# Decoder step on one core: the sample's own cached keys and values read through GpSimd's queue

## The chip, the cores and the metric

The kernel runs on one core of a Trainium2 chip. The core has TensorE (PE in the profile: matmuls and transposes), VectorE (DVE), ScalarE (ACT), GpSimd (POOL) and SyncE (SP, which here only issues transfers), and 16 DMA engines that move data between HBM and on-chip memory. The metric is the device time of one execution in microseconds (us); lower is better.

## The reference, cut to what matters

One inference step of one decoder layer for two groups of tokens that share all weights: a prompt of 1024 tokens and a sample group of 8 sequences with 8 new tokens each. The normalised input goes through one projection, which gives a pooling branch, queries, keys, values and two gates. Attention has three head groups of four heads of 64, with (window, dilation) = (128, 1), (512, 4) and (2048, 16). For a sample token it is

```
idx = Lw + arange(T)[:, None] - arange(band + 1)[None, :] * dil
kg, vg = k_full[:, idxc], v_full[:, idxc]
s = einsum('bthd,btjhd->bthj', q, kg) * HEAD_DIM ** -0.5
p, lse = masked_softmax_stats(s, valid)
out = einsum('bthj,btjhd->bthd', p, vg)
```

where `k_full` and `v_full` are the cached rows followed by the new ones. In the third head group (dilation 16) the 8 new tokens of a sequence share no key: each reads its own 128 cached rows, one in 16. The three groups' outputs are combined by their softmax denominators, mixed with the pooling branch through the gates, projected, and followed by a squared-ReLU MLP. The outputs are both groups' tokens and all updated caches.

## The kernel before, in words

Matrices are f32, split into a high and a low part; a product is three matmul passes. The program runs in this order: the pooling projection, attention (head group index g = 2, then 1, then 0), the gates, the output projections, the MLP. Each head group takes the projection in blocks of 128 tokens: blocks 0 to 7 are the prompt, block 8 is the sample group. For blocks 1 to 5, PE computes queries and keys together (`pqk`, 512 columns) and then values (`pv`); for the others each apart (`pq`, `pk`, `pv`). While PE goes on, a block's queries and keys are normalised in a relay: ACT squares them (L643), DVE sums the squares (L644, `ms`), POOL adds epsilon (L650) and takes the power -1/2 (L651, `mr`), ACT scales (L656), and about one block later PE transposes the result (L672, `tqg1b` for g = 1, `tqg0b` for g = 0).

The third head group's sample attention has no shared keys and does not go to PE. It is done tile by tile while head groups 1 and 0 occupy PE: 16 tiles of keys (`pck`), a softmax, 16 tiles of values (`pcv`). A tile is 128 partitions by 4 cached rows by 256 numbers. `piece` reads it in two halves of 64 partitions (L846); POOL multiplies it in four operations (L856) with the queries or the softmax weights; DVE reduces keys (L869) or adds values (L894, L895). Tiles alternate between two buffers, so tile n + 2 can be read only when DVE has finished tile n. `sample_own_keys` asks for the next tile ahead of multiplying the present one; the multiplications also wait for a matmul that has been traced before them and for the last L651. A tile is worked on after the middle and after the end of a block's PE work, two a block.

At the end, the sums are added into `osm` (L899), combined with the other groups' (L763) and given to PE (L1096). Later POOL also issues 96 cache-to-cache copies (L2115), from 454.9 us on.

PE's order is the order of the program. The order on the other engines and queues is chosen by a scheduler when the kernel is built, from its own estimate of all durations; each engine then runs its list strictly in order, so an instruction that waits holds all behind it. Before the change SyncE's queue issues all transfers but L2115, among them the shared heads' cached keys (`kt`, `keys`, L923 and L927) and the weights (`raw`, L123 and L127).

Of the kernel before, what the change touches and what calls it, by code (L numbers as in the profile page):

```python
# [37 lines left out]
def decoder_step(ctx, tc, i, o):  # L38
    nc = tc.nc
    v_, s_, g_, t_ = nc.vector, nc.scalar, nc.gpsimd, nc.tensor  # L40
    dma = nc.sync.dma_start
# [7 lines left out]
    def rr(p, shape, dt, name, tag, bufs):  # L49

        n = turn[p, tag] = turn.get((p, tag), -1) + 1
        return p.tile(shape, dt, name=name, tag=f"{tag}.{n % bufs}", bufs=1)
# [787 lines left out]
    def piece(kv, j, name):  # L840
        t = rr(sp1, [P, KPC, 256], F32, name=f"pc{name}", tag="pc", bufs=2)
        src = i["cache_kv3"]
        for hf in range(2):
            a = bass.AP(tensor=src.tensor, offset=src.offset + (64 * hf + j) * DIL[2] * NB * 512 + kv * 256,
                        ap=[[512, NT * NB], [DIL[2] * NB * 512, KPC], [1, 256]])
            dma(t[64 * hf:64 * hf + 64], a)  # L846
        return t

    def sample_own_keys(qs, wq):
# [5 lines left out]
        def times(out, *others):  # L855
            ins = g_.tensor_tensor(out, *others, op=ALU.mult)  # L856
            behind_pe(ins)
            behind_pe(ins, last_norm[0])

        loaded = [piece(0, 0, "k0")]  # L860
        yield
        behind_pe(v_.scalar_tensor_tensor(qs[:, :256], wq, HD ** -0.5, qs[:, :256], op0=ALU.mult, op1=ALU.mult))
        for j in js:
            t = loaded.pop()
            loaded.append(piece(0, j + KPC, f"k{j + KPC}") if j + KPC < 64 else piece(1, 0, "v0"))
            for n in range(KPC):
                times(t[:, n], t[:, n], qs[:, :256])
            yield
            behind_pe(v_.tensor_reduce(sc[:, j:j + KPC, :].rearrange("p i h -> p (i h)"),  # L869
                                       t.rearrange("p i (h d) -> p (i h) d", h=4), axis=AX.X, op=ALU.add))  # L870
# [14 lines left out]
        for j in js:  # L885
            t = loaded.pop()
            if j + KPC < 64:
                loaded.append(piece(1, j + KPC, f"v{j + KPC}"))
            for n in range(KPC):
                tv = t[:, n].rearrange("p (h d) -> p h d", h=4)  # L890
                times(tv, tv, sc[:, j + n, :].unsqueeze(2).to_broadcast([P, 4, HD]))
            yield
            if j:
                behind_pe(v_.tensor_tensor(t[:, :2], t[:, :2], t[:, 2:], op=ALU.add))  # L894
                v_.tensor_tensor(st2, st2, t[:, :2], op=ALU.add)  # L895
            else:
                behind_pe(v_.tensor_tensor(st2, t[:, :2], t[:, 2:], op=ALU.add))
# [461 lines left out]
    def row_tile(n, name):  # L1359
        return rr(rows_p, [P, H], F32, name=f"g{n}_{name}", tag=f"g{n}", bufs=2)  # L1360
# [149 lines left out]
    for n, (f, a) in enumerate(order):  # L1510
# [5 lines left out]
        t = row_tile(1 + a, f)  # L1516
# [700 lines left out]
```

## Time and profile before

| what | us |
|---|---|
| median of 3 runs | 1408.12 |
| the runs | 1403.95 to 1409.54 |
| the profiled execution | 1403.42 |
| its span, first to last instruction | 1401.6 |
| PE busy | 1392.2 |
| POOL busy | 236.2 |
| L846 issues on SyncE's queue | 64, from 167.0 to 366.0 |

The page counts an engine as busy while an instruction of it runs. A row of the timeline view has the start, the duration, the engine, the line, the operation and the tiles (output <- inputs); "x4" says how many instructions the row merges, and brackets hold the idle time ahead of it and what ended that. SPq is SyncE's queue; its durations are those of issuing, not of moving data. Waits are listed with their total, their number and the longest.

### The profile page before, as it was taken

What the parts mean: (1) busy time and instruction counts of PE and PEld (TensorE: products, weight loads), DVE (VectorE), ACT (ScalarE), POOL (GpSimd) and SP (SyncE); (2) the same over time, 40 slices, a digit from 0 to 9 for tenths busy, and PEclk for the clock granted to TensorE, in tenths of its full rate; (3) what the DMA queues carried; (4) which work ended last, traced back from release to release, by engine and by line L of the source; (5) the groups of instructions that cost most, each with busy time, mean ns of one, the idle gap of its engine ahead of it and who ended that gap; (6) DMA issues with size and microseconds to landing.
All of it is one profiled execution on the core that took longest, in us unless ns stands there. A gap on an engine that the chain in (4) does not pass through costs nothing.

```text
span 1401.6 us, 29306 instructions
## 1 busy us (share of the span) xinstructions
PE 1392.2 (99%) x11101; PEld 1342.7 (96%) x11101; DVE 954.3 (68%) x1714; ACT 754.5 (54%) x1778; POOL 236.2 (17%) x330
## 2 busy tenths in 40 slices
PE   9999999999999999999999999999999999999998
PEld 8988977887999999999999999999999999999998
DVE  7788744776776767875568677665665686664565
ACT  8557766687765323563336455555554544444443
POOL 0722266475500000000010000000000000000100
PEclk9999999999999999999999999999999999999999
DMA  6322788745477767965368668856758987777684
GB/s 215 117 90 102 220 228 215 216 127 144 120 254 232 253 216 250 319 227 179 130 203 285 227 221 269 269 200 210 249 189 287 325 272 261 234 243 231 206 260 168
DMA packets 184540, 303.57 MB, mean 217 GB/s; under 512 B 26567, under 2 KB 90509, under 8 KB 182350
## 3 DMA queue, kind: packets, MB, share of 16 engines
q1 hardware_dynamic: 181326, 258.04, 58.4%
q0 software_dynamic: 3072, 43.65, 9.8%
q8 instruction: 87, 1.43, 0.4%
q14 instruction: 55, 0.45, 0.1%
HBM read 231.55 MB, written 113.73 MB: 246 GB/s over the span
## 4 chain that ended last, share of the span: by engine, by line
PE 93%; DMA 2%; POOL 2%; DVE 1%; ACT 1%; issue 0%; SPq 0%; DVEq 0%; POOLq 0%
PE pz L1297 24%; PE pd L2075 24%; PE pg L1297 12%; PE ph L200 7%; PE pqk L200 5%; PE pab L1297 5%; PE pv L200 4%; PE a L328 3%; PE pq L200 1%; PE pk L200 1%; POOL pcv L856 1%; PE sg0b L689 1%; PE pog0b L722 1%; PE tpg0b L708 1%; POOL mr L651 0%; DMA ts_d<-ts 0%
## 5 line engine op out<-in xcount | busy, mean ns | idle before, releaser
L2075 PE MATMUL pd<-places 128*128 128x272 f32 x2688 | 331.7, 287 | 0.0
L2075 PEld LDWEIGHTS pd<-places 128*128 128x128 f32 x2688 | 331.6, 188 | 0.0
L116 ACT ACTIVATE places<-raw_d 128x544 fp32r<-128x544 f32 (+1 forms) x176 | 110.7, 646 | 162.7 <-DMA raw_d<-z_d 51.4
L117 DVE TENSOR_TENSOR places<-raw_d,places 128x544 fp32r<-128x544 f32 (+1 forms) x176 | 122.6, 712 | 92.4 <-ACT places L116 90.6
L2115 POOL DMA_DIRECT2D out_kv_sample_dram<-in_cache_kv_dram x96 | 47.2, 492 | 790.7 <-ACT places L116 580.9
L1297 PE MATMUL pz<-act,places 128*128 128x280 f32 (+1 forms) x1080 | 139.4, 287 | 0.0
L1297 PEld LDWEIGHTS pz<-act,places 128*128 128x128 f32 x1080 | 135.9, 188 | 0.0
L200 PE MATMUL ph<-act,places 128*128 128x280 f32 (+1 forms) x768 | 96.6, 287 | 0.0
L200 PEld LDWEIGHTS ph<-act,places 128*128 128x128 f32 x768 | 96.0, 188 | 0.1
L1297 PE MATMUL pg<-act,places 128*128 128x264 f32 (+1 forms) x576 | 75.6, 288 | 0.0
L1297 PEld LDWEIGHTS pg<-act,places 128*128 128x128 f32 x576 | 72.6, 188 | 0.6 <-issue 0.3
L1297 PE MATMUL pz<-places,apart 128*128 128x264 f32 (+1 forms) x528 | 67.9, 287 | 0.0
L1297 PEld LDWEIGHTS pz<-places,apart 128*128 128x128 f32 x528 | 66.6, 188 | 0.0
L200 PE MATMUL pqk<-places,act 128*128 128x512 f32 x240 | 60.6, 402 | 0.6 <-ACT qk L656 0.6
L1297 PE MATMUL pz<-act,apart 128*128 128x264 f32 (+1 forms) x456 | 59.2, 287 | 0.0
L1297 PEld LDWEIGHTS pz<-act,apart 128*128 128x128 f32 x456 | 57.5, 188 | 0.3 <-ACT e L1862 0.2
L200 PEld LDWEIGHTS pqk<-places,act 128*128 128x128 f32 x240 | 44.7, 192 | 10.5 <-ACT qk L656 0.8
L651 POOL TENSOR_TENSOR mr<-ms,mhalf 128x4 f32<-128x4 f32 (+2 forms) x39 | 52.9, 1356 | 3.1
L856 POOL TENSOR_TENSOR pck<-pck,qs 128x256 f32<-128x256 f32 x64 | 47.4, 774 | 29.1 <-DMA pck<-in_cache_kv_dram 24.5
L328 PE MATMUL a<-act,places 128*128 128x384 f32 (+1 forms) x288 | 50.3, 332 | 0.9 <-ACT act L306 0.4
L1297 PE MATMUL pab<-ab,places 128*128 128x264 f32 (+1 forms) x384 | 50.4, 286 | 0.0
L328 PEld LDWEIGHTS a<-act,places 128*128 128x128 f32 x288 | 47.5, 188 | 2.8 <-ACT act L306 1.2
(435 smaller groups left out, 2789.3 us busy)
## 6 DMA issues: line engine op xcount, KB each, us to landing
out_kv_sample_dram<-in_cache_kv_dram POOLq DMA_DIRECT2D x72, 480.0 KB, 4.9
raw_d<-z_d SPq DMA_DIRECT2D x112, 272.0 KB
z_d<-t SPq DMA_DIRECT2D x80, 272.0 KB
raw_d<-in_w_down_dram SPq DMA_DIRECT2D x80, 256.0 KB
raw_u<-in_w_up_dram SPq DMA_DIRECT2D x64, 256.0 KB
raw_qkv<-in_w_in_dram SPq DMA_DIRECT2D x36, 256.0 KB
pck<-in_cache_kv_dram SPq DMA_DIRECT2D x32, 256.0 KB
pcv<-in_cache_kv_dram SPq DMA_DIRECT2D x32, 256.0 KB
```

What stands on the lines that cost most here:

```text
L116: ins = s_.activation(dst_hi, src, AF.Copy)
L117: v_.tensor_tensor(dst_lo, src, dst_hi.bitcast(F32), op=ALU.subtract)
L200: last_mm[0] = t_.matmul(out, lhs(a, k), rhs(b, k), start=(j == 0), stop=(j == len(terms) - 1))
L328: last_mm[0] = t_.matmul(pts[m][:, :n], wt[:, a, kk, m * P:(m + 1) * P], act4[b][kk][:, :, part4(c)], start=(p == 0 and kk == 0), stop=(p ...
L651: last_norm[0] = g_.tensor_tensor(r[:n, :H], ms[:n, :H], mhalf[:n, :H], op=ALU.pow)
L689: t_.matmul(sc[e][:, hp, j * P:(j + 1) * P], qT[rows, hp, :], kT[rows, 2 + hp, :], start=True, stop=True)
L708: t_.transpose(tp[:, hp * nk + j, :], sms[e][:, hp, j * P:(j + 1) * P], ident)
L722: t_.matmul(po[e * HD:(e + 1) * HD, hp, :], vr[:, h * HD:(h + 1) * HD], pTs[e][:, hp * nk + j, :], start=(j == 0), stop=(j == nk - 1))
L856: ins = g_.tensor_tensor(out, *others, op=ALU.mult)
L1297: last_mm[0] = t_.matmul(out[c], lhs(*term), rhs(*term, c), start=(first and n == 0), stop=(n == len(terms) - 1), skip_group_check=not first)
L2075: last_mm[0] = t_.matmul(outs(chain[t], Q)[c], A[:, a, t * P:(t + 1) * P], Z[:, b, c], start=(fresh and f == 0 and n == 0), stop=(f == NG ...
L2115: ins = g_.dma_start(d, a)
```

## The change

The two half-tile reads in `piece` are issued from GpSimd's queue (`g_.dma_start`) instead of SyncE's (`dma`, which is `nc.sync.dma_start`). All else in the source is as it was.

```
@@ piece(kv, j, name)
         for hf in range(2):
             a = bass.AP(tensor=src.tensor, offset=src.offset + (64 * hf + j) * DIL[2] * NB * 512 + kv * 256,
                         ap=[[512, NT * NB], [DIL[2] * NB * 512, KPC], [1, 256]])
-            dma(t[64 * hf:64 * hf + 64], a)
+            g_.dma_start(t[64 * hf:64 * hf + 64], a)
         return t
```

The scheduler places the moved instructions among POOL's and orders DVE, ACT and SyncE anew; PE's order is the same. Three places are spoken of below. In the names, the number at the end tells tiles of one kind apart, and "x4" or "x2" merges equal rows.

The first place is POOL around block 1 of head group 1. Before:

```order
L651 TENSOR_TENSOR mr_0_1_2253<-ms_0_1_2252,mhalf 128x4
L856 TENSOR_TENSOR pck_2172<-pck_2172,qs 128x256 x4
L856 TENSOR_TENSOR pck_2264<-pck_2264,qs 128x256 x4
L856 TENSOR_TENSOR pck_2324<-pck_2324,qs 128x256 x4
L650 TENSOR_TENSOR ms_1_1_2447<-ms_1_1_2447,stats 128x8
L651 TENSOR_TENSOR mr_1_1_2448<-ms_1_1_2447,mhalf 128x8
```

Now:

```order
L651 TENSOR_TENSOR mr_0_1_2253<-ms_0_1_2252,mhalf 128x4
L846 DMA pck_2264<-in_cache_kv_dram 64x4x256 x2
L856 TENSOR_TENSOR pck_2172<-pck_2172,qs 128x256 x4
L856 TENSOR_TENSOR pck_2264<-pck_2264,qs 128x256 x4
L846 DMA pck_2324<-in_cache_kv_dram 64x4x256 x2
L846 DMA pck_2428<-in_cache_kv_dram 64x4x256 x2
L650 TENSOR_TENSOR ms_1_1_2447<-ms_1_1_2447,stats 128x8
L856 TENSOR_TENSOR pck_2324<-pck_2324,qs 128x256 x4
L651 TENSOR_TENSOR mr_1_1_2448<-ms_1_1_2447,mhalf 128x8
```

Ahead of block 1's L651 stand the reads of three tiles, the last of which can be issued only when DVE has reduced pck_2264.

The second place is POOL around block 1 of head group 0, in the values. Before:

```order
L651 TENSOR_TENSOR mr_8_1_3794<-ms_8_1_3793,mhalf 64x4
L856 TENSOR_TENSOR pcv_3767<-pcv_3767,sc 128x256 x4
L650 TENSOR_TENSOR ms_0_1_3855<-ms_0_1_3855,stats 128x4
L651 TENSOR_TENSOR mr_0_1_3856<-ms_0_1_3855,mhalf 128x4
L856 TENSOR_TENSOR pcv_3823<-pcv_3823,sc 128x256 x4
L856 TENSOR_TENSOR pcv_3868<-pcv_3868,sc 128x256 x4
L856 TENSOR_TENSOR pcv_3945<-pcv_3945,sc 128x256 x4
L650 TENSOR_TENSOR ms_1_1_4061<-ms_1_1_4061,stats 128x8
L651 TENSOR_TENSOR mr_1_1_4062<-ms_1_1_4061,mhalf 128x8
```

Now:

```order
L846 DMA pcv_3823<-in_cache_kv_dram 64x4x256 x2
L856 TENSOR_TENSOR pcv_3767<-pcv_3767,sc 128x256 x4
L650 TENSOR_TENSOR ms_0_1_3855<-ms_0_1_3855,stats 128x4
L651 TENSOR_TENSOR mr_0_1_3856<-ms_0_1_3855,mhalf 128x4
L856 TENSOR_TENSOR pcv_3823<-pcv_3823,sc 128x256 x4
L846 DMA pcv_3868<-in_cache_kv_dram 64x4x256 x2
L846 DMA pcv_3945<-in_cache_kv_dram 64x4x256 x2
L856 TENSOR_TENSOR pcv_3868<-pcv_3868,sc 128x256 x4
L856 TENSOR_TENSOR pcv_3945<-pcv_3945,sc 128x256 x4
L650 TENSOR_TENSOR ms_1_1_4061<-ms_1_1_4061,stats 128x8
L846 DMA pcv_4042<-in_cache_kv_dram 64x4x256 x2
L651 TENSOR_TENSOR mr_1_1_4062<-ms_1_1_4061,mhalf 128x8
```

The reads of four tiles have come in between, the last one between L650 and L651.

The third place is ACT at the end of the sample block of head group 1, where PE waits for the scaling of the sample's keys (qk_8):

```order
 L643 ACTIVATE qk_0_2079<-pk_0_2227 128x256
-L656 ACTIVATE qk_8_2077<-pk_8_2179,mr_8_1_2199 64x64 x4
 L663 ACTIVATE v_0_2080<-pv_0_2271,stats 128x256
 L711 COPY pTg2b_0_2305<-tpg2b_0_2302 128x256
+L656 ACTIVATE qk_8_2077<-pk_8_2179,mr_8_1_2199 64x64 x4
+L699 ACTIVATE smg2b_0_2313,sta_697<-smg2b_0_2313,sta_697 128x128 x2
 L656 ACTIVATE qk_0_2079<-pk_0_2227,mr_0_1_2253 128x64 x4
```

That scaling now stands behind two other operations of ACT.

More of the change, by code (lines that the diff above doesn't have):

```diff
@@ L845, in piece @@
                         ap=[[512, NT * NB], [DIL[2] * NB * 512, KPC], [1, 256]])
-            dma(t[64 * hf:64 * hf + 64], a)
+            g_.dma_start(t[64 * hf:64 * hf + 64], a)
         return t
```

## The prediction

> **What bounds the kernel now.** I read the page's first part, then the windows view for the stretch in which the moved reads are issued, then the waits. All times are us.
>
> ```profile
> span 1401.6 us, 29306 instructions
> PE 1392.2 (99%) x11101; PEld 1342.7 (96%) x11101; DVE 954.3 (68%) x1714; ACT 754.5 (54%) x1778; POOL 236.2 (17%) x330
> ```
>
> TensorE (PE) has work in all but 1401.6 - 1392.2 = 9.4. The next row is the stretch 164 to 382, in which the own-key tiles are read and multiplied; after the colon and the length come busy time and instruction count of PE, weight loads, DVE, ACT and POOL, then clock, DMA share and GB/s.
>
> ```profile
> 164.00:382.00 218.00, 215.01 (x1816) 181.81 (x1815) 136.39 (x374) 153.81 (x544) 131.84 (x180) 1.00 0.69 179
> ```
>
> Here PE idles 218.00 - 215.01 = 3.0 in all. That is the most that any edit confined to this stretch can return: 0.2% of the time. POOL works 132 of 218. In the waits (total, times, longest):
>
> ```profile
> PE pog1b L722 <- ACT pTg1b L711: 1.9, 1, 1.9
> ACT qk L656 <- POOL mr L651: 19.8, 19, 3.2
> POOL pck L856 <- DMA pck<-in_cache_kv_dram: 24.5, 10, 5.6
> SPq L846 <- DVE ss L895: 30.2, 10, 7.3
> ```
>
> The last row is what the edit takes from SyncE's queue: it stood 30.2 at the moved reads until DVE had emptied a tile buffer. No wait of PE is put down to a transfer, and none of its idle time in this stretch to SyncE's queue. The second row is what matters instead: ACT often waits for POOL's reciprocal root (mr, L651), scales the new queries and keys (L656), and PE then transposes them (L672). PE has hardly paid for that so far, since there is room ahead of L672; the edit puts its instructions ahead of L651.
>
> **The price of a moved read.** SyncE loses 64 issues, POOL gains 64 (32 tiles, two halves of 64x4x256, 256 KB each). Nothing in this trace shows POOL issuing such a read, so I bound it.
>
> ```profile
> L2115 POOL DMA_DIRECT2D out_kv_sample_dram<-in_cache_kv_dram x96: 488/488/717, 454.9 to 1335.0; - x96
> L846 SPq DMA_DIRECT2D pck<-in_cache_kv_dram x32: 596/608/1007, 167.0 to 256.5; - x32
> 404.10 0.38 SPq L123 DMA_DIRECT2D raw_gf<-in_w_in_dram  x1
> L651 POOL TENSOR_TENSOR mr<-ms,mhalf x39: 1001/1327/2001, 67.0 to 380.1; 128x4 f32<-128x4 f32 x18, 128x8 f32<-128x8 f32 x15, 64x4 f32<-64x4 f32 x6
> ```
>
> (Durations are min/median/max in ns.) The low end is 0.49, POOL's price of a plain copy. On SyncE the moved read costs 0.61 where another read of 256 KB costs 0.38; the same ratio on POOL gives 0.49 x 0.61/0.38 = 0.78, and I take 0.8, since it keeps both the queue and the shape. For the high end I let it stretch as POOL's own small operations do beside other engines (1001 to 2001 ns): 1.56. POOL's added time is 64 x 0.8 = 51, with bounds 31 and 100, on 132 of 218: it fits in sum, so the question is where it delays L651.
>
> The second unknown is landing, from the end of a tile's second issue until both halves are there. For the SyncE reads, POOL's idle time ended by the DMA shows it:
>
> ```profile
> 179.23 1.27 SPq L846 DMA_DIRECT2D pck<-in_cache_kv_dram  x2
> 190.71 1.26 SPq L846 DMA_DIRECT2D pck<-in_cache_kv_dram  x2
> 193.52 1.27 SPq L846 DMA_DIRECT2D pck<-in_cache_kv_dram  x2
> ...
> 178.68 1.01 POOL L651 TENSOR_TENSOR mr<-ms,mhalf 128x4 f32<-128x4 f32 x1
> 179.76 2.82 POOL L856 TENSOR_TENSOR pck<-pck,qs 128x256 f32<-128x256 f32 x4
> 186.61 5.63 POOL L856 TENSOR_TENSOR pck<-pck,qs 128x256 f32<-128x256 f32 x8 [4.02 <-DMA pck<-in_cache_kv_dram]
> 192.48 1.64 POOL L651 TENSOR_TENSOR mr<-ms,mhalf 128x8 f32<-128x8 f32 x1
> 195.45 2.83 POOL L856 TENSOR_TENSOR pck<-pck,qs 128x256 f32<-128x256 f32 x4 [1.33 <-DMA pck<-in_cache_kv_dram]
> 199.37 2.83 POOL L856 TENSOR_TENSOR pck<-pck,qs 128x256 f32<-128x256 f32 x4 [1.09 <-DMA pck<-in_cache_kv_dram]
> ```
>
> 186.61 - 180.50 = 6.1, 195.45 - 191.97 = 3.5 and 199.37 - 194.79 = 4.6: mean 4.7, ends 3.5 and 6.1. I use 4.7 for the new queue too.
>
> The Trainium skill ("DMA: Bandwidth & Descriptors", Specifications) gives the first byte of a GpSimd-issued transfer as about 1 us and of a SyncE-issued one as about 0.6; no run here shows that yet, and as an estimate it would raise the landing to 5.1 and the sum below by some 2.
>
> **Place one: block 1 of head group 1.** The order now has the issues of three tiles ahead of this block's L651, and a multiply that waits for one of them. What L651 feeds:
>
> ```profile
> 189.47 1.22 DVE L869 TENSOR_REDUCE sc<-pck 128x16 f32<-128x1024 f32 x1 [5.63 <-POOL pck L856]
> 194.15 1.75 ACT L656 ACTIVATE qk<-pqk,mr 128x64 f32<-128x64 f32 x8 [3.18 <-POOL mr L651]
> 198.30 0.60 PE L672 MATMUL tqg1b<-cst,qk 128*128 128x128 f32 x4
> ```
>
> From L651's end at 179.7: two issues, 181.3; multiply pck_2172 (2.8), 184.1; pck_2264 has landed at 186.0, multiply, 188.8; issues for pck_2324, 190.4, and for pck_2428, 192.0 (its buffer is free once DVE's 1.22 after 188.8 is done, so no extra wait); pck_2324 lands at 190.4 + 4.7 = 195.1, multiply, 197.9; L651 1.64, 199.5; L656 1.75, 201.3. PE reaches L672 at 198.30: **3.0 late**. With both low ends L656 ends at 197.7 and nothing is late; with both high ends at 207.1, 8.8 late.
>
> **Place two: block 1 of head group 0.** The same, in the values half:
>
> ```profile
> 286.28 1.37 POOL L651 TENSOR_TENSOR mr<-ms,mhalf 64x4 f32<-64x4 f32 x1
> 287.73 3.03 POOL L856 TENSOR_TENSOR pcv<-pcv,sc 128x256 f32<-128x256 f32 x4
> 292.43 2.33 POOL L856 TENSOR_TENSOR pcv<-pcv,sc 128x256 f32<-128x256 f32 x4
> 294.80 0.69 DVE L894 TENSOR_TENSOR pcv<-pcv 128x512 f32<-128x512 f32 x1 [0.63 <-POOL pcv L856]
> 302.28 2.83 POOL L856 TENSOR_TENSOR pcv<-pcv,sc 128x256 f32<-128x256 f32 x4 [3.03 <-DVE natt L601]
> 305.34 1.98 POOL L651 TENSOR_TENSOR mr<-ms,mhalf 128x8 f32<-128x8 f32 x1
> 307.36 1.75 ACT L656 ACTIVATE qk<-pqk,mr 128x64 f32<-128x64 f32 x8 [3.09 <-POOL mr L651]
> 311.95 0.60 PE L672 MATMUL tqg0b<-cst,qk 128*128 128x128 f32 x4
> ```
>
> In this trace's times: 287.7, issues of pcv_3823 289.3, multiply pcv_3767 292.3, L650 and L651 (0.2 and 1.4) 293.9, pcv_3823 landed 294.0 and multiplied 296.3, issues of pcv_3868 297.9, of pcv_3945 299.5 (DVE's two adds of 0.7 free that buffer in time), pcv_3868 landed 302.6, 304.9; pcv_3945 2.8, 307.7; 0.2; issues of pcv_4042 309.5; L651 1.98, 311.5; L656, 313.2: **1.3 late** (0 at the low ends, 9.4 at the high ones).
>
> **Place three, ACT's order.** The first sample scaling (L656, qk_8) now stands behind two other ACT operations, the second (L711) waiting for PE:
>
> ```profile
> 178.03 0.38 PE L708 MATMUL tpg2b<-cst,smg2b 128*128 128x128 f32 x2
> 178.04 0.91 ACT L656 ACTIVATE qk<-pk,mr 64x64 f32<-64x64 f32 x4 [1.63 <-POOL mr L651]
> 179.00 3.02 PE L200 MATMUL pqk<-places,act 128*128 128x512 f32 x12 [0.59 <-ACT qk L656]
> 179.20 0.37 ACT L711 COPY pTg2b<-tpg2b 128x256 f32<-128x256 f32 x1
> ```
>
> 178.4 + 0.4 + 0.9 = 179.7, and PE's pqk starts **0.7 later** than 179.0.
>
> **Elsewhere** I cost the change at nothing. A block's turn of POOL is eight multiplies 5.6, L650 0.2, two issues 1.6, then the later of L651 with two more issues (3.2) and the landing (4.7): 12.1. PE takes longer over a block:
>
> ```profile
> 211.76 0.66 PE L672 MATMUL tqg1b<-cst,qk 128*128 128x128 f32 x4
> 225.96 0.66 PE L672 MATMUL tqg1b<-cst,qk 128*128 128x128 f32 x4
> ```
>
> 14.2, which hides it; at both high ends the turn is 15.1, and that cover is gone. SyncE's remaining reads go out earlier, worth nothing by the waits above. The end of the own-key work has room too: DVE adds its last part at 378.98 and first needs it at 398.81, which is 19 of cover.
>
> ```profile
> 378.98 0.41 DVE L899 TENSOR_TENSOR osm<-osm,ss 128x256 f32<-128x256 f32 x1
> 398.81 1.09 DVE L763 TENSOR_TENSOR osm<-osm,sfe 128x256 f32<-128x256 f32 x3
> ```
>
> Sum: 3.0 + 1.3 + 0.7 = +5.0. The profiled execution took 1403.4, so 1408.4 on its own scale; the three runs shown have a median of 1408.1, 4.7 above it, and I forecast on that scale: 1413.
>
> **The rivals.**
>
> *Hidden* (1408, +0 to +1): both unknowns at their low ends; all three lates vanish but the 0.7. For it: POOL's flat 488 ns. Against: 0.61 on SyncE says that this shape costs more.
>
> *POOL full* (1433, slower): the issue price near 1.56, each read held up by DVE as POOL's roots are. From about 1.3 per issue the lates at places one and two reach 5 each, and POOL's turn nears PE's. At 1.56 and 4.7 the lates are 6.0 and 6.6, with 0.7 and some 3 over the last group's five blocks: +16; at 1.56 and 6.1: 8.8 + 9.4 + 0.7 + 0.9 x 6 + 2 x 5 = +34; I put it midway at +25. For it: the maxima 717 and 2001 ns. Against: medians near the minima.
>
> The Trainium skill ("SBUF — State Buffer", SBUF: two separate sides) says that descriptors of a GpSimd-issued DMA cannot be written while VectorE runs a two-port operation; it is this rival's mechanism, and its figure, some 620 ns becoming 3100, would put the time beyond that rival's upper end.
>
> *Freed SyncE* (1405, faster): its queue stood 30.2 and everything behind moves up; if PE's 3.0 of idle time go and POOL hides its issues, -3. For it: 30.2. Against: every wait of PE in the stretch ended at ACT.
>
> **How the numbers follow.** Changes below 0.5% (7 us) cannot be told from none with this kernel. Forecast 0.52 (within 0.36, slower 0.16, since at a price of 1.0 the same sums give 3.8 + 2.5 + 0.7 = 7.0), hidden 0.20 (within 0.18, faster 0.02), POOL full 0.22 (slower), freed SyncE 0.06 (half faster, half within). That makes faster 0.05, within 0.57, slower 0.38. The range 1404 to 1430 holds the first two, most of the last, and POOL full up to +22.
>
> **What would show it.** Right: L846 on POOL at 0.7 to 0.9; L656 of block 1 (group 1) waiting for L651 until about 199, and idle time of PE ahead of L672 there and 114 later; PE's idle time in the stretch grown from 3 to about 8. Wrong: issues above 1.3, PE idle in most blocks, DVE waiting for L856 at length; or PE's idle time unchanged.

## The result, and the profile after

| | us |
|---|---|
| before, median of 6 runs | 1406.45 (1403.95 to 1409.54) |
| after, median of 6 runs | 1415.16 (1413.66 to 1417.09) |
| ratio, with its 95% interval | 1.0064 [1.0054, 1.0075] |
| profiled execution, before and after | 1403.42 and 1417.09 |

The change makes the kernel slower: by 8.7 us between the medians, by 0.64% in the ratio. The forecast of 1413 was 2 us short, but what had been given the highest chance, a change within 0.5%, was not what came, and the experiments show that most of the loss did not come from where the sum put it. The two profiled executions are 13.7 apart, since that of before is faster than all of its six runs and that of after is its slowest; the differences between traces below are somewhat too large for that reason.

The page of after, first part:

```profile
span 1415.3 us, 29282 instructions
PE 1397.3 (99%) x11101; PEld 1345.6 (95%) x11101; DVE 960.6 (68%) x1714; ACT 754.6 (53%) x1778; POOL 275.1 (19%) x394
```

PE's idle time went from 9.4 to 1415.3 - 1397.3 = 18.0, so 8.6 of the 13.7 are idle time. The other 5.1 are busy time (1392.2 to 1397.3) for the same 11101 matmuls: some of them ran at a lower clock. The windows view of after for the stretch in which the reads are issued shows both:

```profile
164.00:382.00 218.00, 208.02 (x1701) 173.56 (x1700) 133.91 (x352) 145.87 (x518) 161.40 (x231) 0.98 0.66 173
```

PE idles 10.0 there, where it idled 3.0, and its mean clock is 0.98 instead of 1.00. What a read costs GpSimd stands in the view of line L846 (durations min/median/max in ns, first and last start in us), with the time from issue to landing:

```profile
L846 POOL DMA_DIRECT2D pck<-in_cache_kv_dram x32: 619/619/808, 159.6 to 273.6; - x32
L846 POOL DMA_DIRECT2D pcv<-in_cache_kv_dram x32: 619/619/684, 282.8 to 379.9; - x32
DMA to landing us min/median/max: 3.3/4.6/9.8
```

0.62 an issue, and a median landing of 4.6 from an issue's start: the forecast took 0.8 and 4.7, the latter from the end of a tile's second issue (counted so, the 32 tiles have a median of 4.2 and a longest of 9.2). But the longest landing is 9.8, and the first issue is at 159.6; on SyncE it was at 167.0. From the waits of after (total, times, longest):

```profile
PE pog2b L722 <- ACT pTg2b L711: 3.0, 1, 3.0
PE pqk L200 <- ACT qk L656: 2.1, 1, 2.1
PE pss L970 <- DMA keys<-in_kT_dram: 1.4, 1, 1.4
PE tqg0b L672 <- ACT qk L656: 1.2, 1, 1.2
ACT qk L656 <- POOL mr L651: 22.5, 16, 2.9
POOL pck L856 <- DMA pck<-in_cache_kv_dram: 18.2, 11, 6.2
DVE osm L1164 <- DMA ts_d<-ts: 2.6, 1, 2.6
```

The two largest stalls are at the opening of head group 1, and neither is at place one or two. The third is a wait of PE for a transfer that is still on SyncE's queue (`keys`, at 223.8); before, no wait of PE was for a transfer. The three places of the prediction, in the timeline of after:

```profile
184.70 4.62 PE L200 MATMUL pqk<-places,act 128*128 128x512 f32 x12 [2.08 <-ACT qk L656]
201.45 1.71 ACT L656 ACTIVATE qk<-pqk,mr 128x64 f32<-128x64 f32 x8
205.58 0.60 PE L672 MATMUL tqg1b<-cst,qk 128*128 128x128 f32 x4
315.13 1.25 POOL L846 DMA_DIRECT2D pcv<-in_cache_kv_dram  x2
316.39 2.21 POOL L651 TENSOR_TENSOR mr<-ms,mhalf 128x8 f32<-128x8 f32 x1
320.96 0.96 PE L672 MATMUL tqg0b<-cst,qk 128*128 128x128 f32 x4 [1.17 <-ACT qk L656]
```

Place three is the first row: pqk starts 5.7 later than before and takes 4.62 instead of 3.02. Place one is the next two: ACT ends at 203.2, and PE arrives at 205.58, without a stall, since it is 7.3 late by then. Place two is the rest, with a stall of 1.17 where 1.3 was forecast.

To compare kernels below I use how much later than before PE starts the first transposes (L672) of five blocks in the profiled execution. Before, these start at 182.81 (block 0 of head group 1, "opening"), 198.30 (its block 1), 275.27 (its block 6, the last but one), 311.95 (block 1 of head group 0) and 386.98 (its last). Each row rests on one execution.

| kernel | opening | block 1 | block 6 | block 1 of g = 0 | last of g = 0 | ratio of times |
|---|---|---|---|---|---|---|
| after | +7.3 | +7.3 | +7.7 | +9.0 | +12.3 | 1.0064 [1.0054, 1.0075] |
| e1: first four reads only | +4.6 | +4.6 | +3.1 | +3.4 | +3.4 | 1.0035 [1.0019, 1.0052] |
| e2: the other 60 only | +0.2 | +3.7 | +3.4 | +6.9 | +8.5 | 1.0073 [1.0056, 1.0089] |
| e3: first four held back | +6.9 | +6.9 | +6.6 | +9.8 | +12.2 | 1.0074 [1.0058, 1.0089] |
| e4: values only | +0.1 | +0.5 | +0.2 | +1.1 | +6.0 | 1.0041 [1.0028, 1.0054] |
| e5: first multiply put off | +3.2 | +3.1 | +5.4 | +9.1 | +11.5 | 1.0063 [1.0045, 1.0080] |
| e6: the same, reads on SyncE | +0.3 | +0.3 | +2.4 | +2.0 | +1.5 | 1.0002 [0.9990, 1.0013] |
| e7: put off, first four on SyncE | -0.2 | -0.2 | +2.4 | +5.6 | +8.1 | 1.0045 [1.0030, 1.0059] |
| e8: only GpSimd made busy | +4.3 | +4.3 | +4.8 | +8.9 | +8.6 | 1.0033 [1.0020, 1.0046] |
| e9: reads moved, old order held | +4.3 | +5.9 | +13.7 | +17.8 | +23.6 | 1.0170 [1.0152, 1.0188] |
| e10: reads on SyncE, new order held | +1.5 | +1.5 | -1.1 | -1.2 | -0.7 | 0.9992 [0.9976, 1.0009] |
| e11: GpSimd busy, old order held | +1.3 | +2.7 | +8.8 | +10.7 | +11.9 | 1.0056 [1.0042, 1.0070] |
| e12: GpSimd busy, new order held | +1.3 | +1.5 | -0.8 | +1.1 | +1.4 | 0.9990 [0.9982, 0.9999] |

### The profile page after: what moved, and what is told of

Read it like the earlier page. It is cut to its first block, busy times and chain, and to the rows that moved or that the text cites. A ratio compares the mean times of both kernels' runs of the same rounds, so it can differ in the third digit from the quotient of the medians.

```text
span 1415.3 us, 29282 instructions
## 1 busy us (share of the span) xinstructions
PE 1397.3 (99%) x11101; PEld 1345.6 (95%) x11101; DVE 960.6 (68%) x1714; ACT 754.6 (53%) x1778; POOL 275.1 (19%) x394
## 3 DMA queue, kind: packets, MB, share of 16 engines
q1 hardware_dynamic: 163918, 241.26, 53.3%
q0 software_dynamic: 8192, 60.43, 14.4%
## 4 chain that ended last, share of the span: by engine, by line
PE 83%; DMA 6%; POOL 5%; DVE 2%; ACT 2%; issue 1%; SPq 1%; DVEq 0%; POOLq 0%; ACTq 0%
PE pz L1297 24%; PE pd L2075 23%; PE pg L1297 11%; PE ph L200 7%; PE pab L1297 4%; PE a L328 3%; PE pqk L200 3%; PE pv L200 2%; POOL pcv L856 1%; DMA pcv<-in_cache_kv_dram 1%; DMA pck<-in_cache_kv_dram 1%; POOL mr L651 1%; POOL pck L856 1%; PE pk L200 1%; DMA keys<-in_kT_dram 1%
## 5 line engine op out<-in xcount | busy, mean ns | idle before, releaser
L200 PEld LDWEIGHTS pqk<-places,act 128*128 128x128 f32 x240 | 45.7, 196 | 12.3 <-ACT qk L656 2.3
L651 POOL TENSOR_TENSOR mr<-ms,mhalf 128x4 f32<-128x4 f32 (+2 forms) x39 | 53.9, 1382 | 2.2
L856 POOL TENSOR_TENSOR pck<-pck,qs 128x256 f32<-128x256 f32 x64 | 47.6, 775 | 22.2 <-DMA pck<-in_cache_kv_dram 18.2
```

What stands on the lines that cost most here:

```text
L200: last_mm[0] = t_.matmul(out, lhs(a, k), rhs(b, k), start=(j == 0), stop=(j == len(terms) - 1))
L651: last_norm[0] = g_.tensor_tensor(r[:n, :H], ms[:n, :H], mhalf[:n, :H], op=ALU.pow)
```

## Which reads cost: e1 to e4

The trace of after leaves two suspects for the opening: the first four reads, which now leave before the last weights, and the new order of the engines' work. Later blocks lose more. So I moved parts of the reads.

**e1**, only the first two tiles' reads on GpSimd:

```
-            dma(t[64 * hf:64 * hf + 64], a)
+            (g_.dma_start if (kv, j) in ((0, 0), (0, KPC)) else dma)(t[64 * hf:64 * hf + 64], a)
```

> The kernel before with only the first four reads (the first two tiles of the keys) issued by GpSimd; the other 60 stay with SyncE. Theory A (the reads leave too early): on GpSimd these four leave at 159.6 instead of 167.0 and meet the last weight panels, so PE idles about 3 ahead of L722 at 165 and its clock falls for some us: +4 to +7, a time of 1410 to 1414. Theory B (GpSimd's issue time in the relay to PE costs): four issues of 0.62 at a place where POOL is idle cost nothing, 1406 to 1407.

Measured: 1409.93 (before beside it 1405.58), at the lower edge of theory A. Four reads of 64 cost some 4 us, all at the opening, and nothing is lost after that.

**e2**, the other 60, with `not in` in the same condition:

> The changed kernel with the first four reads given back to SyncE; 60 stay with GpSimd. Theory A: PE's idle time ahead of L722 at 165 is gone and the clock there is 1.00; what is left is the head group 0 part, +2 to +5, a time of 1408 to 1411. Theory B: nearly all of the +8.7 stays, 1413 to 1415.

Measured: 1415.72, as slow as the whole change, so theory A missed. The opening is on time (+0.2), and now the stall that the prediction had at place one is there. The timelines of e2, PE and ACT:

```profile
200.58 1.75 ACT L656 ACTIVATE qk<-pqk,mr 128x64 f32<-128x64 f32 x8 [5.15 <-POOL mr L651]
201.98 1.31 PE L672 MATMUL tqg1b<-cst,qk 128*128 128x128 f32 x4 [3.29 <-ACT qk L656]
```

ACT waits 5.15 for L651 and PE 3.29 for ACT; 3.0 had been worked out. So place one is real, and in after it is hidden by the 7.3 that PE has already lost. The losses of e1 and e2 do not add: whoever is late first gives the relay behind it room.

**e3**, the first four held in GpSimd's list until ACT has split the last weight panel that the opening needs (`behind_pe` here makes one instruction wait for another; the last edit, one line in the kernel, is written out over three):

```
-                behind_pe(ins, ends_of[p["key"]])
+                behind_pe(ins, ends_of[p["key"]]); last_split[0] = ins
...
-            g_.dma_start(t[64 * hf:64 * hf + 64], a)
+            ins = g_.dma_start(t[64 * hf:64 * hf + 64], a)
+            if (kv, j) in ((0, 0), (0, KPC)):
+                behind_pe(ins, last_split[0])
```

> The changed kernel, all 64 reads on GpSimd, with the first two tiles' reads held until ScalarE has taken the last of the weight panels that PE needs next (L116, 163.9 in the trace of before). Theory A: no idle time ahead of L722, clock 1.00, 4 less than the changed kernel or more: 1408 to 1411. Theory B: 1414 to 1416, since every issue is still on POOL.

Measured: 1416.70, above both ranges. It gained nothing, but it moved the stall, as two rows of its timelines (DVE, PE) show:

```profile
177.72 0.43 DVE L862 SCALAR_TENSOR_TENSOR qs<-wq,qs 128x256 f32<-128x256 f32 x1 [4.75 <-DMA wq<-in_qk_norm_dram]
183.72 5.23 PE L200 MATMUL pqk<-places,act 128*128 128x512 f32 x12 [5.92 <-ACT qk L656]
```

The stall for weights at L722 is gone, and DVE waits instead for the small read `wq`, which SyncE's queue issues after the weights and which now flies beside the four reads. POOL's first multiply waits for DVE, L651 stands behind the multiply, and PE stalls 5.92. In after and in e3 alike, the four leave ahead of their old place in SyncE's queue and delay something that stood ahead of them there.

**e4**, only the 32 reads of values (`g_.dma_start if kv else dma`):

> Only the 32 reads of the values are issued by GpSimd, the keys' stay with SyncE. In the profiles the changed kernel falls a further 4.3 behind between L672 of block 0 and the last block of head group 0. If that is made by the values' own issues (both theories): about 1411, with PE idle ahead of L672 of block 1 of head group 0. If it is left over from the new order in the keys' half: 1406 to 1408.

Measured: 1411.37. Of the 6.0 that PE is late in the profiled execution, 4.3 come at one place, between blocks 2 and 3 of head group 0. The timelines of POOL and DVE there:

```profile
321.83 1.27 POOL L846 DMA_DIRECT2D pcv<-in_cache_kv_dram  x2
332.56 2.33 POOL L856 TENSOR_TENSOR pcv<-pcv,sc 128x256 f32<-128x256 f32 x4 [3.48 <-DMA pcv<-in_cache_kv_dram]
334.92 0.69 DVE L894 TENSOR_TENSOR pcv<-pcv 128x512 f32<-128x512 f32 x1 [2.63 <-POOL pcv L856]
```

The tile's second issue ends at 323.10, and both halves have landed at 332.56: 9.5. POOL multiplies, DVE's add (L894) waits for that, and behind the add stands L972, for which PE waits 2.16. PE's clock then falls to 0.52 (the window 337 to 340). Place two shows 0.99 in e4 and 1.17 in after, against 1.3.

## Is it the order? e5 to e7

The scheduler puts the first multiply (L856) ahead of the roots of the opening blocks. In e5 the own-key work after the first read request is put off by one step, on top of the change; e6 is the same put-off with the reads on SyncE, as a control; e7 has the put-off and only the 60 later reads on GpSimd.

```
             loaded.append(piece(0, j + KPC, f"k{j + KPC}") if j + KPC < 64 else piece(1, 0, "v0"))
+            yield from range(j == 0)
```

> The changed kernel with the first own-key multiply put off by one step, so that in POOL's order the two roots (L651) that the head group 1 sample block and block 0 need stand ahead of it; all later own-key work moves on by one step too. Theory C (a paced or data-waiting own-key instruction stands ahead of a root in POOL's in-order queue): PE's wait ahead of pqk (2.08 in the changed kernel) and the slow matmuls behind it go, what is left of the early reads is the 3 to 4 ahead of L722: 1409 to 1413. Theory D (POOL's time for 64 issues): no change, 1414 to 1416.

> The control to it: the same put-off, all reads on SyncE. Both theories: like the kernel before, 1404 to 1408.

> The put-off with the first four reads on SyncE and 60 on GpSimd. Theory C: no early reads and no root behind a waiting multiply, so PE is not late before head group 0; what is left is the values' part (5.8 in the run with the values alone): 1409 to 1412. Theory D: 1414 to 1416.

Measured: 1414.07, 1406.52 and 1412.10 (before 1405.66); e5 missed the range of theory C. The put-off costs nothing by itself (e6). It takes 4 us from the opening (e5: +3.2), and by the end of the groups all but 0.8 of them are lost again. e7 starts both the opening and block 1 on time and is 8.1 late at the end (6.4 in its median). So neither the early departure nor place one is needed for a loss of this size: the later reads can make it alone, in small stalls at many places.

Slow landings are not peculiar to GpSimd's queue. In before, with SyncE issuing, a tile's second issue ends at 210.61 and POOL has both halves at 218.68, 8.1 later:

```profile
209.34 1.27 SPq L846 DMA_DIRECT2D pck<-in_cache_kv_dram  x2
218.68 2.99 POOL L856 TENSOR_TENSOR pck<-pck,qs 128x256 f32<-128x256 f32 x4 [0.66 <-DMA pck<-in_cache_kv_dram]
```

Counted in the same way, the longest of after is 9.2. On both queues the landing goes with how busy the DMA engines are meanwhile. Taken from the end of a tile's first issue to 5 us behind its second, their share is above 0.95 for 9 of the 32 tiles of after, which land in 6.6 on average, and the other 23 land in 4.0. Of the 13 tiles of before for which POOL waited, the 8 above 0.95 land in 6.0 and the other 5 in 3.7.

## Is it GpSimd's time? e8

Before, with all reads on SyncE, and beside each issue one operation on a spare tile on GpSimd:

```
             dma(t[64 * hf:64 * hf + 64], a)
+            g_.tensor_tensor(idle_t, idle_t, mhalf[:, :2], op=ALU.pow)
```

> The kernel before, all reads on SyncE, with a small power operation on a spare 128x2 tile on GpSimd beside each of the 64 issues: about 0.6 to 0.7 of POOL's time each, in about the places of the moved issues, but without a transfer, a buffer wait or a landing behind it. The spare tile feeds nothing. Theory D (POOL's time is what costs): +4 to +8, 1410 to 1414. Theory A or C (late or colliding transfers and waits in POOL's queue): 1405 to 1408.

Measured: 1411.16. An operation takes 0.70, much like an issue, and no read is moved, yet 5.5 us are lost, more than half of the change's 8.7. I read this as GpSimd's time costing half. That reading did not stand: the scheduler knows of the 64 operations and makes an order of its own for e8, which is neither that of before nor that of the change: the 64 operations run from 161.9 to 283.4, and not at the places of the moved issues, the last of which is at 379.9. The last four runs hold it.

## Order, time and reads taken apart: e9 to e12

The names of all instructions of VectorE, ScalarE, GpSimd and SyncE, in the order of before or of the change, are written into the kernel as a table, and each is tied to the one behind it by an edge that sets the order and adds no wait on the chip:

```
+    for row in _ORDER:
+        for a, b in zip(row, row[1:]):
+            tc.add_manual_dep(traced[b], a, edge, reason="hold")
```

e9 has the reads on GpSimd and the order of before; the scheduler places the 64 issues into it. e10 has the reads on SyncE and the order of the change. In e11 and e12 the reads are on SyncE, and an operation as in e8 stands in GpSimd's order at each place where e9 (for e11) or the changed kernel (for e12) has an issue.

> All 64 reads on GpSimd as in the change, but every other instruction of VectorE, ScalarE, GpSimd and SyncE is held in the order that it had before. If the new order of the work on the engines is what costs the 8.7 us, this kernel is back at 1405 to 1409. If it is what the reads do on GpSimd itself (64 issues of 0.62 us in its one queue, late landings, transfers meeting others), 1412 to 1416, with head group 1 opening 4 to 7 us later than before. A result between, 1409 to 1412, shares the loss.

> All 64 reads on SyncE as before, but every other instruction is held in the order that the changed kernel has. If the new order is what costs, 1411 to 1415, with head group 1 late although GpSimd issues nothing. If it is the issuing on GpSimd, 1405 to 1408 and TensorE idle near the 9.4 us of before. If only the reads' early start at the head of head group 1 costs, the same 1405 to 1408, since on SyncE they start behind the weights again.

> The order of before is held on VectorE, ScalarE, GpSimd and SyncE, all 64 reads are on SyncE, and at each place in GpSimd's order at which the kernel with the held old order issued a read there stands one operation on a spare tile of about 0.69 us (an issue takes 0.62). It reads no new data and waits for no buffer. If the time that the issues take in GpSimd's order is the cause, this is near that kernel's 1428, at least 1420. If it is the reads themselves (an issue that waits in GpSimd's queue for its buffer, landings that come late), it is 1404 to 1410. In between, the loss is shared in that proportion.

> The same with the order of the changed kernel: its instructions stand on every engine in its order, the reads are on SyncE, and in place of each of the 64 issues GpSimd runs one operation of about 0.69 us. If the time of the issues is the cause, 1411 to 1416, with head group 1 opening about 7 us late. If the transfers are (sent early, meeting other reads, landing late), 1402 to 1407. The kernel with its own plan and such operations lost 5.5 us; about half would be 1408 to 1411.

Measured, in us (before beside e9 and e10: 1405.27; beside e11 and e12: 1406.19):

| | order of before | order of the change |
|---|---|---|
| reads on SyncE | 1405.27 (before itself) | 1403.24 (e10) |
| reads on SyncE, GpSimd busy at the issues' places | 1413.66 (e11) | 1404.23 (e12) |
| reads on GpSimd | 1428.39 (e9) | 1415.16 (after) |

Three things follow.

*The new order costs nothing*: e10 is within 0.5% of before, and if anything on the fast side. It is not what makes the change slow; it is what keeps it from being far slower. Without it (e9) the same reads cost 1.7%, outside all that I had expected of e9.

*GpSimd's time costs nothing in the new order, and 7.5 us in the old one.* The row of e12 for 278 to 382, with the busy time of POOL as the fifth number after the colon and the length, stands against that of after:

```profile
278.00:382.00 104.00, 102.03 (x844) 88.29 (x845) 74.69 (x200) 80.88 (x265) 86.60 (x118) 1.00 0.46 124
```

```profile
278.00:382.00 104.00, 100.72 (x806) 86.46 (x805) 74.03 (x185) 78.60 (x262) 82.46 (x118) 1.00 0.49 124
```

POOL is busier in e12 than in after (86.60 against 82.46, with 118 instructions in each), and PE idles 2.0 instead of 3.3.

*The rest is the reads themselves*: 1415.16 - 1404.23 = 10.9 in the new order, 1428.39 - 1413.66 = 14.7 in the old one. After and e12 run the same lists on the four engines, with the operations of e12 at the very places of the issues, so their rows can be laid side by side. The opening in after (ACT, ACT, PE, DVE, POOL, and the write of `ts` on SyncE's queue):

```profile
164.31 0.63 ACT L116 ACTIVATE places<-raw_qkv 128x512 fp32r<-128x512 f32 x1 [3.71 <-DMA raw_qkv<-in_w_in_dram]
167.28 0.63 ACT L116 ACTIVATE places<-raw_qkv 128x512 fp32r<-128x512 f32 x1 [2.34 <-DMA raw_qkv<-in_w_in_dram]
168.22 0.74 PE L722 MATMUL pog2b<-pTg2b,v 128*64 128x128 f32 x6 [2.97 <-ACT pTg2b L711]
174.20 0.28 DVE L1164 MEMSET osm<- 64x264 f32 x1 [2.65 <-DMA ts_d<-ts]
179.53 2.92 POOL L856 TENSOR_TENSOR pck<-pck,qs 128x256 f32<-128x256 f32 x4 [3.23 <-PE pv L200]
L533 SPq DMA_DIRECT2D ts_d<-ts x1: 525/525/525, 163.7 to 163.7; - x1
```

and in e12:

```profile
163.61 1.33 ACT L116 ACTIVATE places<-raw_qkv 128x512 fp32r<-128x512 f32 x2 [2.76 <-DMA raw_qkv<-in_w_in_dram]
169.31 0.28 DVE L1164 MEMSET osm<- 64x264 f32 x1 [0.69 <-DMA ts_d<-ts]
175.23 2.80 POOL L856 TENSOR_TENSOR pck<-pck,qs 128x256 f32<-128x256 f32 x4 [3.82 <-PE tpg2b L708]
L533 SPq DMA_DIRECT2D ts_d<-ts x2: 525/525/525, 149.8 to 163.1; - x2
180.28 3.02 PE L200 MATMUL pqk<-places,act 128*128 128x512 f32 x12 [2.17 <-ACT qk L656]
```

With the four reads on their way from 159.6 on, the second weight panel comes at 167.28 instead of 164.3: ACT's copy for L722 stands behind it, and PE stalls 2.97. The clock then falls to 0.61 (the window 168 to 171), and PE is 4.5 late when it ends the `pv` matmuls for which POOL's first multiply waits: that multiply starts at 179.53 instead of 175.23. L651 and L656 stand behind it, so pqk starts at 184.70 instead of 180.28, 4.4 later, and then runs at a lower clock for another 1.6.

The write of `ts`, which has to be over before DVE may overwrite its place (L1164), ends 10.5 after its issue instead of 6.2 (174.20 - 163.7; 169.31 - 163.1). DVE's product `qs` (L862), which the same multiply needs, stands behind L1164 and is there at 179.3. This delay alone would have made pqk nearly as late; PE's own, at 179.5, ends last.

The rows of before show what the four reads run into (the last three numbers are clock, DMA share and GB/s):

```profile
157.00:160.00 3.00, 3.00 (x26) 2.94 (x25) 3.00 (x7) 2.94 (x10) 0.00 (x0) 1.00 0.08 20
160.00:163.00 3.00, 3.00 (x28) 3.00 (x27) 1.39 (x5) 0.38 (x1) 0.00 (x0) 1.00 0.93 247
163.00:165.00 2.00, 2.00 (x22) 1.77 (x20) 1.68 (x4) 1.67 (x5) 0.00 (x0) 1.00 1.04 404
```

Up to 160 the DMA engines are nearly idle; from then on, when the reads now leave, they are full with the last weights: little room for a megabyte that comes sooner.

In head group 0 the losses are of e4's kind. After, POOL and DVE, where e12 has no wait of POOL for a read:

```profile
329.79 1.27 POOL L846 DMA_DIRECT2D pcv<-in_cache_kv_dram  x2
339.00 2.36 POOL L856 TENSOR_TENSOR pcv<-pcv,sc 128x256 f32<-128x256 f32 x4 [2.98 <-DMA pcv<-in_cache_kv_dram]
341.39 0.69 DVE L894 TENSOR_TENSOR pcv<-pcv 128x512 f32<-128x512 f32 x1 [2.14 <-POOL pcv L856]
342.11 0.28 DVE L972 TENSOR_TENSOR p<-pss,cst 128x136 f32<-128x136 f32 x1
```

331.06 to 339.00 is a landing of 7.9, POOL idles 2.98, DVE 2.14, and L972 behind it makes PE wait 0.76. The DMA share is 0.96 and 1.08 in the two windows from 326 to 334. How long POOL waits for reads in all does not tell the loss: 33.7 in before and 33.6 in e10, which lose nothing, against 24.4 in after. What counts is what stands behind such a wait. In e9, where the lists were not made for it, this is worse, and a read that waits for its buffer also holds a root. DVE's waits and POOL's timeline in e9 (the profile puts the wait down to L972, which DVE runs right behind the reduction L869 that frees the buffer):

```profile
DVE sc L869 <- POOL pck L856: 35.0, 10, 9.8
DVE pcv L894 <- POOL pcv L856: 19.0, 7, 7.2
```

```profile
209.14 1.23 POOL L846 DMA_DIRECT2D pck<-in_cache_kv_dram  x2 [1.08 <-DVE p L972]
210.37 1.66 POOL L651 TENSOR_TENSOR mr<-ms,mhalf 128x8 f32<-128x8 f32 x1
```

By place, the profiled executions of after and e12 divide the loss so: at the last block after is 12.3 - 1.4 = 10.9 later, and 7.3 - 1.3 = 6.0 of that is there at the opening, for which only the first four reads had been issued (the fifth leaves at 184.64, just before pqk starts). The other 4.9 come behind. What stays open: what the other 60 would cost in this order if the first four were left on SyncE, since being late gives the relay room. e1 and e2 moved them apart, but each with an order of its own, and e8 shows what that can do. It is also open whether the queue of GpSimd shares the DMA engines as well as SyncE's does at equal traffic: of before, only the reads for which POOL waited can be timed.

## Why the prediction came close, and where it was wrong

- *What bounds the kernel*: right. Nothing but PE's idle time and its clock changed the end, and no gain came from the freed SyncE, as costed. That its queue stood 30.2 at the moved reads is one row of ten: the ten rows of L846 add up to 52.7.
- *The price of a moved read*: 0.62 instead of 0.8, so 64 x 0.62 = 40 on GpSimd instead of 51. The scaling by 0.61/0.38 overdid it; GpSimd issues this read at the price at which SyncE does. The high end of 1.56 rests on a misreading: 1001 to 2001 ns mixes shapes, and L651 on 128x4 alone goes from 1007 to 1582 in before, which would have put the high end at 1.2.
- *Landing*: the 4.7 was near the median (4.2, counted alike). The high end of 6.1 was too low: the longest is 9.2, and the stalls hang on the longest ones. The trace of before could have told, since the three waits used are of 13 and the longest landing among these is 8.1. The first-byte figure of the Trainium skill ("DMA: Bandwidth & Descriptors", Specifications) did not raise the median. In the working above, 5.1 instead of 4.7 would have added 1.2 to the sum and not 2.
- *Place one, +3.0*: right in size (e2: 3.29), though in after it cost nothing, because PE was late already. It is not GpSimd's time that makes it: with the issues' time alone in the same order, e12 loses 0.2 between the opening and block 1. It takes reads that leave late in GpSimd's list and are then waited for, which the working did contain: in e2 POOL waits 3.3 and 2.7 for them ahead of L651.
- *Place two, +1.3*: right; 1.17 in after, and no stall there in e12, where GpSimd is as busy and issues no read.
- *Place three, +0.7*: this step failed, in size and in cause. The opening lost 7.3, not 0.7. The new order, of which the 0.7 was made, costs 1.5 there (e10), and not by ACT's list: L711 is over at 176.4 in e10, and L656 then waits for GpSimd's root, which stands behind the first multiply (175.41 instead of 173.94 in before). The reads add the rest: weights and `ts` come later, and the clock falls. ACT in e10:

```profile
179.51 0.91 ACT L656 ACTIVATE qk<-pk,mr 64x64 f32<-64x64 f32 x4 [3.13 <-POOL mr L651]
```

- *Elsewhere, nothing*: this step failed too. It costed what GpSimd and SyncE issue, and never asked what the first four reads meet when they leave at 159.6 instead of 167.0, nor what a landing of 8 to 10 does to DVE's order. Behind place two, after loses 12.3 - 9.0 = 3.3 more, and in head group 1 it waits 1.4 for `keys`.
- *The rivals*: hidden fell. POOL full fell as stated: issues are at 0.62, the longest at 0.81, and the lock that the Trainium skill describes ("SBUF — State Buffer", SBUF: two separate sides) does not show in them. Its size (1433) is near e9's 1428, but by another mechanism. Freed SyncE fell. Of the signs named for the forecast, only the stall at place two came as stated: the issues are below 0.7 to 0.9, L656 of block 1 does not wait for L651 in after, and PE's idle time in the stretch is 10.0 and not about 8.
- *The sum*: the median came out 8.7 above before, where 5.0 was forecast. Of the 5.0 only place two is found in after as it was put; the agreement of the totals is in good part luck, since place one was absorbed by a larger loss that the sum did not have. The forecast of 1413 also started from 1408.1, the median of three runs; with all six it is 1406.45, and the same +5.0 would have given 1411.5.

The rule of the Trainium skill that would have given the missing step stands in "DMA: Bandwidth & Descriptors", Issuing engines are not separate DMA queues: transfers of all issuing engines run on the same 16 DMA engines and interleave, so another issuer only saves sequencer time. The trace agrees: in after, the weights and the write of `ts` on SyncE's queue come 3.0 and 4.3 later than in e12 once four reads of GpSimd's queue fly beside them.

## What to carry to other kernels

A queue that issues in order is also a schedule for the DMA engines: a transfer taken out of it no longer waits behind the ones that were ahead, and where the DMA engines are nearly full these pay for it. Before moving transfers to another queue, find the earliest time at which each can now leave and list what else is flying then; and remember that on a compute engine's queue a read leaves only when that engine gets to it, and one that waits for its buffer holds the engine's own work too. To tell the cost of an engine's time from that of the transfers, put idle operations in the place of the issues and hold the order, because a scheduler that sees other durations writes another program.

## What the runs showed of the hardware

**Clock.** The prediction has no term for PE's granted clock. It falls after short stalls, and not after each. In after it falls behind the stall of 2.97 at L722, and again behind that of 2.08, after which the twelve matmuls of pqk take 4.62. The windows have a clock of 0.61 and 0.72 (seventh number):

```profile
168.00:171.00 3.00, 2.78 (x16) 2.52 (x17) 2.42 (x6) 1.58 (x7) 0.00 (x0) 0.61 1.04 351
184.00:190.00 6.00, 5.30 (x21) 3.74 (x22) 3.02 (x10) 3.65 (x19) 5.34 (x8) 0.72 0.36 98
```

In e12 the same matmuls behind a stall of 2.17 take 3.02, at full clock (its row is above). So a stall of 2 us can cost 3.7, and its length alone does not tell. The Trainium skill ("TensorE: Matmul & The Clock Gate", Part 1: The HAM clock gate) has the clock halved after an idle window of about 3.4 us, in windows that run freely. That two stalls of the same length end differently agrees with free-running windows; that 2.08 or 2.97 is enough does not agree with a whole idle window.

**Packets.** The same 16.78 MB are 5120 packets on GpSimd's queue (8192 - 3072) where they were 17408 on SyncE's (181326 - 163918), so 3.3 KB instead of 0.96 KB each. The DMA queues of after (packets, MB, packet time as a share of 16 engines' span), and those of before:

```profile
q1 hardware_dynamic: 163918, 241.26, 53.3%
q0 software_dynamic: 8192, 60.43, 14.4%
```

```profile
q1 hardware_dynamic: 181326, 258.04, 58.4%
q0 software_dynamic: 3072, 43.65, 9.8%
```

In microseconds, since the spans differ, 64 of packet time leave SyncE's queue (58.4% of 1401.6 less 53.3% of 1415.3) and 66 come to GpSimd's (14.4% of 1415.3 less 9.8% of 1401.6): the larger packets did not make the reads cheaper for the DMA engines.
